# A matrix product by two levels of Strassen-Winograd: A's tiles transposed as 32-bit words, two opening pairs stored, a12's product by the second level in more places

## The chip, the core and the metric

The kernel runs on one core of one Trainium2 chip. Its engines work side by side and meet through semaphores: TensorE (PE, matmuls, with weight loads of its own beside them), VectorE (DVE), ScalarE (ACT), GpSimd (POOL, which here issues the DMAs that turn fp32 into fp16) and SyncE (SP, which issues all other DMAs). The time is device microseconds of one execution; the kernel before has a median of 1470.02 us over 3 runs.

## The reference

```python
def reference(a, b, bias):          # a, b: 4096 x 4096 fp32, bias: 4096 fp32
    return np.tanh(np.matmul(a, b) + bias)
```

The kernel computes in fp16 on PE with fp32 sums.

## The kernel before

**Products.** The output is made in four chunks of 1024 columns (`c` = 0 to 3). A row block is 128 rows of A, a *pair* two of them, a *duo* two pairs. Of a pair, the quadrants a11, a12, a21, a22 are one row block by half of k each; a quadrant is a buffer of 16 k-tiles of 128 x 128. The first level makes seven products of a pair instead of eight: P1 = a11 b11, P2 = a12 b21, P3 = s4 b22, P4 = a22 t4, P5 = s1 t1, P6 = s2 t2, P7 = s3 t3, where s1 = a21 + a22, s2 = s1 - a11, s3 = a11 - a21, s4 = a12 - s2 and t1 to t4 are the same kind of sums of B's quadrants. A *plain* product (`product`, line 726) is 16 matmuls of 512 columns per pair, so 32 per duo. A *fine* one (`fine_product`, line 741, called by `fine` and by the class `Fine`) takes the duo's two pairs together and uses the same scheme once more: seven times 8 matmuls of 256 columns, 56 per duo, with sums of its own: y and z of the left tiles on DVE (`fine_left`), f1 to f4 of the right ones (`fine_right`).

**Stages.** The opening multiplies the first eight row blocks (pairs 0 to 3, buffers `o00` to `o71`) by chunk 0 with plain matmuls in an order written out by hand (lines 1468 to 1511): tiles landing by DMA (`land`), PE, results put aside and taken up again by DVE (`take_up`). Then chunk 0 goes through duos 2 to 7 (`run_duo`), which load A by POOL (`natural`). Chunks 1 to 3 have two passes each (`pass_one`, `pass_two`) over all eight duos: P1, P2 and, in chunks 2 and 3, P6 in the first; P7, P6, P5, P4, P3 in the second. `SECONDS` says in how many duos of the first pass P2 (a12's product) is fine. What a first pass leaves for the second goes to DRAM as a state, but for the last duo, whose state stays on chip.

**Where A comes from.** POOL's DMA reads fp32 rows and writes fp16 into `land` or `nat`, with each 32 partitions holding a quarter of k. DVE then transposes 32 x 32 blocks of it (`transpose`, line 455) into k-tiles, so that k lies on the partitions. A left tile of a matmul is 128 neighbouring fp16 elements per partition. Which k goes to which partition must agree with B's rows: `load_b` reads B with rows `dx` apart per partition and `dt` per tile; for the first four k-tiles `dx` is 4, else 1, and `transpose` makes up for it by a separate instruction. The pairs in `early` (4 to 15) are stored in DRAM in chunk 0 as fp16 tiles (`keep`, names in `BASIS`) and fetched by SP afterwards; pairs 0 to 3 are loaded and transposed once more in chunk 1 (`upper`, `others`).

**The order of the work.** A planner (class `Plan`) takes all operations with a guessed duration, ranks them by a due time and lays them out for each engine; PE's order is that of the program, that of DVE, ACT, POOL and SP comes out of the plan, as does the place in SBUF of each buffer (51 large places). An engine works its queue strictly in that order. `soft` makes an operation due at the latest so long after what it needs.

The planner's guesses for DVE and ACT:

```python
def dve(n, emit, reads, writes, wide=False, **kw):
    add("DVE", 0.15 + n / (960 if wide else 1900), emit, reads, writes, **kw)
def act(n, emit, reads, writes, **kw):
    add("ACT", 0.17 + n / 1200, emit, reads, writes, **kw)
```

Of the kernel before, what the change touches and what calls it, by code (L numbers as in the profile page):

```python
# [10 lines left out]
P = 128  # L11
QP = 32
# [3 lines left out]
T = 16  # L16
TB = 4
# [4 lines left out]
fp16 = mybir.dt.float16  # L22
ADD = mybir.AluOpType.add
# [14 lines left out]
LATER = 6  # L38
PLAIN = (0, 0, 0, 0)
# [4 lines left out]
SECONDS = (0, 4, 6, 8)  # L44
# [81 lines left out]
class Plan:  # L126
    LATE = 0.1
# [235 lines left out]
def kernel(  # L363
# [91 lines left out]
    def transpose(dst, src, h=1, t0=0):  # L455

        nt = src.shape[-1] // QP
        split = [(0, nt, "P mb (t x) -> P mb t x")]
        if h == 0 and t0 == 0:
            split = [(0, TB, "P mb (x t) -> P mb t x"), (TB, nt - TB, split[0][2])]  # L460
        for t, n, order in split:
            nc.vector.transpose(  # L462
                dst[:, ds(t, n), :].rearrange("P t (mb p) -> P mb t p", p=QP),
                src[:, :, ds(t * QP, n * QP)].rearrange(order, x=QP),
            )

    def turn_time(n, h=1, t0=0):
        return (0.34 if h == 0 and t0 == 0 else 0.17) + n * 0.00103
# [11 lines left out]
    def natural_rows(pair, r, s, soft=SOFT):  # L480

        pq = [s.setdefault(f"a{r + 1}{h + 1}", new(f"a{r + 1}{h + 1}", [P, T, P], atoms=2)) for h in range(2)]
        for u in range(2):
            tl = new("nat", [P, 2, 2 * T * QP])

            def srcs(q, u=u):
                src = a[ds((2 * pair + r) * P + u * 2 * QP, 2 * QP), ds(q * KQ, KQ)]
                return src.rearrange("(mb p) k -> p mb k", p=QP), ()

            load_rows(tl, srcs, P * T * P * 4)  # L490
            for h, dst in enumerate(pq):

                def emit(dst=dst, tl=tl, u=u, h=h):
                    transpose(dst[ALL, ALL, ds(u * 2 * QP, 2 * QP)], tl[ALL, ALL, ds(h * T * QP, T * QP)], h)

                add("DVE", turn_time(1024, h), emit, (tl,), ((dst, (u,)),), soft=soft)

    def natural(pair, kept, own=False, few=False):
        s = {}
        for name in ("a11", "a22", "a21", "a12") if few else ():  # L500
            r, h = int(name[1]) - 1, int(name[2]) - 1
            tl = new("nat", [P, 4, T * QP])
            s[name] = new(name, [P, T, P], atoms=2)

            def srcs(q, r=r, h=h):
                src = a[ds((2 * pair + r) * P, P), ds(q * KQ + h * T * QP, T * QP)]
                return src.rearrange("(mb p) k -> p mb k", p=QP), ()

            load_rows(tl, srcs, P * T * P * 4)
            for u in range(2):  # L510

                def emit(dst=s[name], tl=tl, u=u, h=h):
                    transpose(dst[ALL, ALL, ds(u * 2 * QP, 2 * QP)], tl[ALL, ds(2 * u, 2), ALL], h)

                add("DVE", turn_time(1024, h), emit, (tl,), ((s[name], (u,)),))
        for r in () if few else range(2):
            natural_rows(pair, r, s, 0.0)
# [46 lines left out]
    def asum(s, name, x, y, op, over=None):  # L564
        x, y = s[x], s[y]
        s[name] = s[over] if over else new(name, [P, T, P], atoms=2)
        tt(at(s[name]), at(x), at(y), op, T * P, (x, y), (s[name],), wide=False)
# [1045 lines left out]
```

## Time and profile before

| what | value |
|---|---|
| time of 3 runs | 1470.02 us (median), 1469.94 to 1472.13 us |
| the profiled execution | 1469.58 us |
| its span on the core | 1467.9 us |
| granted TensorE clock, mean | 0.998 |
| DMA | 394.33 MB, mean 269 GB/s |
| HBM | 321.39 MB read, 146.54 MB written |

Lines of the profile name an instruction by the line of the program, its engine, its operation and the tiles that it writes and reads (buffer numbers left out). All sums on DVE have line 427, all copies on ACT line 430, the DMAs of A on POOL line 476, those of B line 660, DVE's transposes line 462. "xN" is a count, "mean ns" the mean of one.

### The profile page before, as it was taken

The page shows a single profiled execution, that of the slowest core. Times are in us where ns is not written, and L with a number is a line of the kernel's source. Part 1 is how long each engine was busy: PE and PEld are TensorE (multiplying, and loading weights), DVE is VectorE, ACT ScalarE, POOL GpSimd, SP SyncE. Part 2 cuts the span into 40 slices and gives each one's busy share as a digit, 9 for nine tenths or more (in the row PEclk, how much of TensorE's full clock was granted, in tenths as well). Part 3 has the DMA queues.
Part 4 walks back from the last instruction along what each step waited for, and adds up shares of the span by engine and source line. Part 5 has one row for each costly group of instructions (what it writes and reads, how often), then busy time and mean ns, then how long its engine had stood idle before and what let it go on. Part 6 is the DMA issues. An engine that isn't in the chain of part 4 may idle for free.

```text
span 1467.9 us, 28245 instructions
## 1 busy us (share of the span) xinstructions
PE 1454.4 (99%) x10848; PEld 1060.9 (72%) x10848; DVE 1174.2 (80%) x1835; ACT 439.7 (30%) x990; POOL 310.8 (21%) x581
## 2 busy tenths in 40 slices
PE   9999999999999999999999999999999999999998
PEld 4444545555478566667778878888888888888887
DVE  4669897778688978888789889887778878987765
ACT  2111211221123222433334322244343332243433
POOL 8764334334333011200120300000111210000000
PEclk9999999999999999999999999999999999999999
DMA  9999999999999999999999999588999988778772
GB/s 177 179 220 268 200 255 259 230 229 246 233 274 309 315 281 321 325 340 353 312 289 379 286 327 319 188 295 275 270 291 357 264 239 271 247 233 284 250 252 102
DMA packets 201751, 394.33 MB, mean 269 GB/s; under 512 B 27408, under 2 KB 74512, under 8 KB 201616
## 3 DMA queue, kind: packets, MB, share of 16 engines
q1 hardware_dynamic: 126864, 316.99, 61.7%
q0 software_dynamic: 74752, 75.53, 32.5%
q8 instruction: 85, 1.39, 0.4%
q14 instruction: 50, 0.41, 0.1%
HBM read 321.39 MB, written 146.54 MB: 319 GB/s over the span
## 4 chain that ended last, share of the span: by engine, by line
PE 94%; DMA 3%; POOL 2%; DVE 1%; issue 1%; ACT 0%; DVEq 0%; POOLq 0%; SPq 0%
PE ps L748 60%; PE ps L733 29%; PE ps L1417 5%; DMA b<-in_b_dram 1%; POOL b L660 1%; DMA a<-a 1%; POOL land L476 1%; DMA out_dram<-cs 0%; DMA land<-in_a_dram 0%; DMA out_dram<-parts 0%; POOL first L1344 0%; DVE parts L427 0%; DVE ps L427 0%; DVE t L427 0%; DVE ya L427 0%
## 5 line engine op out<-in xcount | busy, mean ns | idle before, releaser
L660 POOL DMA_DIRECT2D b<-in_b_dram x256 | 137.5, 542 | 560.1 <-DVE ps L427 198.0
L476 POOL DMA_DIRECT2D nat<-in_a_dram x256 | 136.2, 537 | 303.7 <-PE ps L748 91.2
L430 ACT COPY ps<-ps 128x256 f32<-128x256 f32 (+1 forms) x257 | 94.2, 366 | 329.0 <-PE ps L748 316.4
L733 PEld LDWEIGHTS <-s 128*128 128x128 f16 x1056 | 103.3, 98 | 115.9
L462 DVE STREAM_TRANSPOSE a<-nat 128x256 f16<-128x256 f16 (+2 forms) x192 | 155.2, 859 | 30.3 <-PE ps L733 18.8
L733 PEld LDWEIGHTS <-a 128*128 128x128 f16 x896 | 87.4, 98 | 100.5 <-DVE a L427 0.8
L748 PEld LDWEIGHTS <-a 128*128 128x128 f16 x1320 | 129.2, 98 | 25.4 <-issue 1.4
L733 PE MATMUL ps<-b,a 128*128 128x512 f16 x640 | 143.6, 379 | 0.0
L748 PEld LDWEIGHTS <-zs 128*128 128x128 f16 x1248 | 122.1, 98 | 16.0
L748 PEld LDWEIGHTS <-ys 128*128 128x128 f16 x1248 | 122.1, 98 | 14.1
L733 PE MATMUL ps<-t,s 128*128 128x512 f16 x576 | 129.2, 379 | 0.0
L748 PEld LDWEIGHTS <-ya 128*128 128x128 f16 x1136 | 111.1, 98 | 14.8 <-DVE ya L427 1.5
L748 PEld LDWEIGHTS <-za 128*128 128x128 f16 x1136 | 111.2, 98 | 13.7 <-issue 0.2
L430 ACT COPY parts<-ps 128x256 f32<-128x256 f32 (+1 forms) x166 | 65.0, 392 | 171.1 <-PE ps L748 86.9
L1417 PE MATMUL ps<-b,o 128*128 128x512 f16 x512 | 113.1, 383 | 2.4 <-DVE ps L427 2.3
L733 PE MATMUL ps<-b,s 128*128 128x512 f16 x480 | 110.9, 379 | 0.0
L427 DVE TENSOR_TENSOR parts<-ps,parts 128x256 f32<-128x256 f32 (+1 forms) x156 | 68.9, 442 | 43.2 <-PE ps L748 28.4
L448 ACT ACTIVATE parts<-ps 128x512 f32<-128x512 f32 x64 | 38.2, 597 | 201.6 <-PE ps L733 135.2
L1417 PEld LDWEIGHTS <-o 128*128 128x128 f16 x512 | 50.3, 99 | 63.8 <-issue 5.1
L427 DVE TENSOR_TENSOR ps<-ps,parts 128x256 f32<-128x256 f32 (+1 forms) x171 | 76.2, 447 | 21.8 <-PE ps L748 16.8
L748 PE MATMUL ps<-b,a 128*128 128x256 f16 x656 | 85.0, 273 | 1.1 <-ACT ps L430 1.1
L748 PEld LDWEIGHTS <-xs 128*128 128x128 f16 x736 | 72.0, 98 | 10.1 <-issue 1.2
(118 smaller groups left out, 2478.3 us busy)
## 6 DMA issues: line engine op xcount, KB each, us to landing
a<-a SPq DMA_DIRECT2D x74, 512.0 KB, 7.0
a<-a SPq DMA_DIRECT2D x148, 256.0 KB, 6.5
b<-in_b_dram POOLq DMA_DIRECT2D x256, 128.0 KB, 7.6
nat<-in_a_dram POOLq DMA_DIRECT2D x256, 128.0 KB, 7.5
out_dram<-parts SPq DMA_DIRECT2D x112, 256.0 KB, 5.8
ys<-s SPq DMA_DIRECT2D x46, 512.0 KB, 4.5
xs<-s SPq DMA_DIRECT2D x46, 512.0 KB, 5.1
s<-s SPq DMA_DIRECT2D x38, 512.0 KB, 5.9
```

The costliest lines, as they stand in the source:

```text
L427: dve(n, lambda: nc.vector.tensor_tensor(out=o(), in0=x(), in1=y(), op=op), reads, writes, wide, **kw)
L430: act(n, lambda: nc.scalar.copy(o(), x()), reads, writes, **kw)
L448: act(NB, lambda: nc.scalar.activation(o[ALL], src[ALL], TANH), (src,), (o,), soft=2.0)
L462: nc.vector.transpose(dst[:, ds(t, n), :].rearrange("P t (mb p) -> P mb t p", p=QP), src[:, :, ds(t * QP, n * QP)].rearrange(order, x=QP),)
L476: nc.gpsimd.dma_start(out=tl[(ds(q * QP, QP), *key)], in_=src)
L660: nc.gpsimd.dma_start(out=dst.rearrange("p t j n -> p t (j n)") if j is None else dst, in_=src)
L733: nc.tensor.matmul(bank[ALL], left[ALL, k + t, ALL], rb.tile(t), start=start and k == t0 and t == 0, stop=k + t == t0 + nt - 1, skip_group ...
L748: nc.tensor.matmul(bank[ALL, HALF[half]], buf[ALL, at_ * TP + i * TB + t, ALL], rb.tile(t), start=False, stop=i == 1 and t == TB - 1, skip ...
L1417: nc.tensor.matmul(bank[ALL], left[ALL, t, ALL], rb.tile(tb), start=start, stop=stop, skip_group_check=True,)
```

## The change

1. `transpose` looks at the fp16 source as 32-bit words, pairs of neighbouring k, and transposes words. Two k-tiles then lie interleaved in the buffer: word m of a partition holds element m of the one tile and element m of the next. One instruction does what took two in the first half of k; every transpose has half as many elements, of twice the width. A left tile is 128 fp16 elements at a step of two (`left_tile`). `load_b` reads all of B with rows four apart per partition, and the opening's copies behind PE's transposes write at a step of two (`pairs_of`).
2. `natural` always loads a quadrant at a time, which before it did for the first three duos; the later ones had whole rows of k.
3. After the opening, s1 and s2 of pairs 0 and 1 (`FIRST`) are formed from the opening's buffers and a11, a12, a22, s2 are stored in DRAM. In chunk 1 these pairs are fetched as the others are.
4. `SECONDS` goes from (0, 4, 6, 8) to (0, 8, 8, 8): the P2 of four more duos in chunk 1 and two more in chunk 2 is fine.
5. The planner's guesses: DVE's fixed part 0.15 to 0.08, ACT's 0.17 to 0.09, a transpose from 0.17 + 0.00103 n (0.34 where there were two) to 0.09 + 0.00052 n, the time between engines (`LATE`) 0.1 to 0.18.
6. `HOLD` says how many states stay on chip, one in each chunk. `third` would form s3 again from a22 and s2 for pairs whose s3 is not in `held_names`; `others` enters it there for every pair.

```diff
-SECONDS = (0, 4, 6, 8)
+SECONDS = (0, 8, 8, 8)
+HOLD = (1, 1, 1, 1)
+FIRST = (0, 1)
+HELD = ("s1", "s3", "s4")
 class Plan:
-    LATE = 0.1
+    LATE = 0.18
...
-        add("DVE", 0.15 + n / (960 if wide else 1900), emit, reads, writes, **kw)
+        add("DVE", 0.08 + n / (960 if wide else 1900), emit, reads, writes, **kw)
-        add("ACT", 0.17 + n / 1200, emit, reads, writes, **kw)
+        add("ACT", 0.09 + n / 1200, emit, reads, writes, **kw)
...
+    def transpose(dst, src, t0=0, row0=0):
+        src = src.bitcast(pair32)
+        nu, nmb = src.shape[-1] // QP, src.shape[1]
+        nc.vector.transpose(
+            dst[ALL].rearrange("P t m -> P (t m)").bitcast(pair32).rearrange("P (U m) -> P U m", m=P)[
+                :, ds(t0 // 2, nu), ds(row0, nmb * QP)
+            ].rearrange("P (v u) (mb p) -> P mb v u p", p=QP, u=2),
+            src.rearrange("P mb (v x u) -> P mb v u x", x=QP, u=2),
+        )
+    def turn_time(n):
+        return 0.09 + n * 0.00052
+    def pairs_of(buf, t):
+        return buf[ALL, ds(t, 2), ALL].rearrange("P a b -> P (a b)").rearrange("P (m e) -> P e m", e=2)
+    def left_tile(buf, t):
+        return pairs_of(buf, t - t % 2)[:, t % 2]
...
     def load_b(buf, c, k0, nt, j=None, early=0.0):
-        dx, dt = (1, QP) if k0 >= TB else (TB, 1)
...
+                    ap=[[TB * N, QP], [N, nt], [1, n]],
...
-                        bank[ALL], left[ALL, k + t, ALL], rb.tile(t),
+                        bank[ALL], left_tile(left, k + t), rb.tile(t),
...
-                        bank[ALL, HALF[half]], buf[ALL, at_ * TP + i * TB + t, ALL], rb.tile(t),
+                        bank[ALL, HALF[half]], left_tile(buf, at_ * TP + i * TB + t), rb.tile(t),
...
-                eng, 0.35, lambda t=t, fn=fn: fn(aq[m, 0][ALL, ds(t, 2), ALL], box["tp"][:, ds(t, 2), :]),
+                eng, 0.35, lambda t=t, fn=fn: fn(pairs_of(aq[m, 0], t), box["tp"][:, ds(t, 2), :]),
...
+    for p in FIRST:
+        s = {f"a{r + 1}{h + 1}": aq[2 * p + r, h] for r in range(2) for h in range(2)}
+        asum(s, "s1", "a21", "a22", ADD, soft=2.0)
+        asum(s, "s2", "s1", "a11", SUB, over="s1", soft=2.0)
+        keep(p, s)
     finish_bias(k0)
...
-    early = {4, 5, 6, 7, 8, 9, 10, 11, 12, 13, 14, 15}
+    early = set(range(4, NP)) | set(FIRST)
...
-            d.a = [natural(p, p in early, i == 0, i < 3) for p in d.pairs]
+            d.a = [natural(p, p in early, i == 0) for p in d.pairs]
```

More of the change, by code (lines that the diff above doesn't have):

```diff
@@ L22 @@
 fp16 = mybir.dt.float16
+pair32 = mybir.dt.uint32
 ADD = mybir.AluOpType.add
@@ L518, in natural @@
+    def natural(pair, kept, own=False):
+        s = {}
+        for name in ("a11", "a22", "a21", "a12"):
+            natural_tile(pair, name, s)
         if own:
```

133 lines of the change are left out of this document (70 added, 63 removed).

## The prediction

> **What bounds the kernel now.** I read the page first: its span, the engines' busy times and the chain that ended last.
>
> ```profile
> span 1467.9 us, 28245 instructions
> ...
> PE 1454.4 (99%) x10848; PEld 1060.9 (72%) x10848; DVE 1174.2 (80%) x1835; ACT 439.7 (30%) x990; POOL 310.8 (21%) x581
> ...
> PE 94%; DMA 3%; POOL 2%; DVE 1%; issue 1%; ACT 0%; DVEq 0%; POOLq 0%; SPq 0%
> ```
>
> TensorE (PE) is busy 99% of the span and owns 94% of the chain, so the time is PE's work plus its few waits. The chain in order of time gives the pace of that work, and the waits of PE name who ended each of them (us in total, times, longest).
>
> ```profile
> 615.76 6.91 PE ps L733 x32
> 628.75 12.23 PE ps L748 x112
> ```
>
> ```profile
> PE ps L1417 <- DVE ps L427: 2.3, 1, 2.3
> PE ps L748 <- DVE ps L427: 1.6, 3, 0.8
> ...
> PE ps L748 <- DVE ya L427: 1.3, 1, 1.3
> PE ps L748 <- ACT ps L430: 1.1, 1, 1.1
> ```
>
> 32 plain matmuls of 512 columns (line 733) take 6.91 us, 216 ns each; 112 matmuls of 256 columns (line 748, the second level) take 12.23 us, 109 ns each. Nothing stands between them: weight loads are hidden. Two things can move the time: the count of matmuls, and about 6.3 us of waits, of which one, 2.3 us, is in the opening and 4.0 us (1.6 + 1.3 + 1.1) in the rest.
>
> **The change part by part.**
>
> *a12's product.* A duo's plain product is 32 matmuls, 6.91 us; by the second level it is 56, half of 12.23, 6.12 us. Chunk 1 goes from 4 to 8 such duos, chunk 2 from 6 to 8: six duos of 0.79 us, **-4.75 us**. Nothing hides PE, so this comes off the end unless new waits eat it.
>
> *Strided weights.* Every left tile is now read at a step of two elements, and each matmul has a load of its own. Today the loads have step one, except in the sixteen opening transposes on PE, whose source is read at a step of four:
>
> ```profile
> L748 PEld LDWEIGHTS <-a 128*128 128x128 f16 x1320 | 129.2, 98 | 25.4 <-issue 1.4
> ```
>
> ```profile
> L1455 PEld LDWEIGHTS <-first x16: 111/113/137, 9.1 to 11.4; 128*128 128x128 f16 x16
> ```
>
> ```profile
> 9.80 0.41 PE L1455 MATMUL tp<-ident,first 128*128 128x128 f16 x4 [0.30 <-DMA first<-in_a_dram]
> ...
> 10.05 0.59 PE L1417 MATMUL ps<-b,o 128*128 128x512 f16 x2
> ```
>
> A load takes 98 ns dense and 113 ns at step four, and 113 is more than the 109 ns of a 256-column matmul. But four such loads with four 128-column matmuls go from 9.80 to 10.05, 62 ns a pair: the loads overlap each other. A pair at 62 ns fits into 109. Price between 0 and +4 ns x some 8,680 small matmuls, 35 us; I take 0, since 62 ns is a rate and 113 only a latency. The page "TensorE: Matmul & The Clock Gate" of the Trainium skill (section "Weight-path perf modes — Fast Weight Load (FWL) and DoubleRow") says that the fast load reads 32 bits at a time, which speaks against a step that uses one half of each word, and elsewhere allows strided columns. By the first reading the loads would lose their speed and the 35 us rival below would come; the row at step four, which uses a quarter of each 8 bytes, bears out the second.
>
> *Transposes as words.* VectorE (DVE) now moves half as many elements, by one instruction where two were.
>
> ```profile
> L462 DVE STREAM_TRANSPOSE a<-nat 128x1024 f16<-128x1024 f16 x64 | 76.7, 1217 | 11.1 <-PE ps L733 9.5 <-PE ps L748 1.3
> ...
> L427 DVE TENSOR_TENSOR parts<-ps,parts 128x256 f32<-128x256 f32 x144 | 60.7, 422 | 40.7 <-PE ps L748 28.4 <-ACT ps L430 4.9 <-ACT cs L1086 4.4
> L462 DVE STREAM_TRANSPOSE a<-nat 128x768 f16<-128x768 f16 x64 | 59.9, 935 | 0.0
> ...
> L427 DVE TENSOR_TENSOR st<-st,p 128x512 f32<-128x512 f32 x48 | 32.5, 686 | 1.1
> ...
> L427 DVE TENSOR_TENSOR ya<-ya,a 128x1024 f16<-128x1024 f16 x41 | 28.2, 689 | 1.0
> ...
> L462 DVE STREAM_TRANSPOSE a<-nat 128x256 f16<-128x256 f16 x64 | 27.1, 424 | 19.2 <-PE ps L733 9.3 <-DMA nat<-in_a_dram 5.9 <-PE ps L748 3.9
> ...
> L462 DVE STREAM_TRANSPOSE o<-land 128x2048 f16<-128x2048 f16 x8 | 18.1, 2294 | 3.5 <-DMA land<-in_a_dram 2.3 <-PE ps L1417 1.2
> ...
> L462 DVE STREAM_TRANSPOSE o<-land 128x512 f16<-128x512 f16 x12 | 7.5, 680 | 11.3 <-DMA land<-in_a_dram 11.3
> ...
> L1461 DVE COPY o<-tp 128x256 f16<-128x256 f16 x4 | 1.0, 286 | 9.1 <-PE tp L1455 9.1
> ```
>
> No row has a transpose of words. 512 words lie between 424 ns (the 256-element row, if two words went at once) and 1217 ns (1024 half-words, if bytes counted). I take 680: 512 elements of either width take that, transposed (680) or added (686). The 192 transposes of `nat` (76.7 + 59.9 + 27.1 = 163.7 us) become 112 of 0.68, 76 us; the eight long ones of the opening fall from 2294 to the 1217 of 1024 elements, 9 us less. DVE gets some 96 us back, but it is off the chain: worth only what its waits cost. The copies behind PE's transposes (286 ns) now write at step two; at the pace of the 424 row two of them take 0.3 us more, before 12 us, and the stage paced by loads that follows (below) hides it.
>
> *DVE's new work.* Each new fine product costs four half-tile sums (0.69), two bank sums (0.42) and two adds of the state (0.69): 5.0 us, 30 us for six. ACT gets four copies more a duo, at 30% busy (page). The two pairs' s1 and s2 are four sums of 2048 elements, twice the 1024 row or 5.5 us at most, in the opening.
>
> *The opening.* PE's 2.3 us wait is here.
>
> ```profile
> 51.85 2.37 DVE L462 STREAM_TRANSPOSE o<-land 128x1024 f16<-128x1024 f16 x2 [1.37 <-DMA land<-in_a_dram]
> 54.15 4.87 DVE L427 TENSOR_TENSOR ps<-spill,bias 128x512 f32<-128x512 f32 x8
> ```
>
> ```profile
> 40.00:60.00 20.00, 17.67 (x75) 7.50 (x73) 9.54 (x12) 4.20 (x8) 15.71 (x29) 0.91 1.24 185
> ```
>
> (Columns of a stretch: its length, busy time of PE, weight loads, DVE, ACT and POOL, the granted clock of PE, DMA.) The first take-up of a bank (54.15) stands behind two transposes that wait for a landing at 51.85. In the changed kernel's instruction order that take-up comes ahead of them, so the wait should go, and with it the slow clock behind it: 0.91 granted over 20 us, 1.8 us. Together at most 4.1 us. Against it stand the stores of the two pairs: 4 MB on SP, of which 1 MB (a11 of row blocks 0 and 2) leaves around the bias load, before some 45 us.
>
> ```profile
> 80.99 1.58 POOL L660 DMA_DIRECT2D b<-in_b_dram  x3 [0.73 <-DMA b<-in_b_dram]
> ...
> 88.34 5.11 POOL L476 DMA_DIRECT2D land<-in_a_dram  x8 [0.18 <-issue]
> ...
> 103.63 0.54 POOL L476 DMA_DIRECT2D nat<-in_a_dram  x1 [0.81 <-DMA nat<-in_a_dram]
> ```
>
> ```profile
> b<-in_b_dram POOLq DMA_DIRECT2D x256, 128.0 KB, 7.6
> ...
> out_dram<-parts SPq DMA_DIRECT2D x112, 256.0 KB, 5.8
> ```
>
> ```profile
> 92.15 0.60 ACT L448 ACTIVATE parts<-ps 128x512 f32<-128x512 f32 x1 [35.58 <-PE ps L1417]
> ```
>
> POOL's queue of loads paces this stage. From 88.34 eight loads go at 0.64 us each; at 103.63, while outputs of 256 KB are stored, one takes 0.81 + 0.54 = 1.35. So a 256 KB store costs the loads up to 0.7 us, 1 MB 2.8 us. The last block of b is issued by 82.57 and, at the median of 7.6 us, lands by 90; PE is through with its first use at 92.15, when ACT gets the first result. That is 2 us of slack: of the 4.1 gained, less 2.8 lost, little is left. The other 3 MB leave between 90 and 120 us beside the first duo's loads, up to 8 us of their time.
>
> ```profile
> 131.59 2.36 DVE L462 STREAM_TRANSPOSE a<-nat 128x1024 f16<-128x1024 f16 x2
> ```
>
> ```profile
> 139.43 13.98 PE L733 MATMUL ps<-t,s 128*128 128x512 f16 x64
> ```
>
> a22 of the second pair is transposed by 133.95, and the product that needs its sums begins at 139.43, its second half 3.5 us later: some 6 to 9 us of slack less two sums (2.5), which the stores may use up. Then PE waits for s2. So the opening gives between -4.1 and +3 us; nearer to the gain, since the wait that goes is a row and the stores may find gaps, I take **-1.5**. SP issues in order: its bias load now stands behind the first store, which waits for row block 0's transposes, and the bias is first read at 54.15; outputs behind a later store wait for the sums that it waits for, and their buffers come back later to ACT, which is 30% busy. Both I cost at nothing.
>
> *Fewer loads in chunk 1, and what does nothing.* Pairs 0 and 1 come back from DRAM as half-words: 32 POOL loads of 128 KB go, and SP's load issues take their place. Smaller rows in the loads of the first chunk's last three duos (2 KB for 4 KB) and other row steps in the loads of b are hidden: PE's waits name no load behind the opening. I cost them at nothing; without that cover one load late is 1.35 us. One state on chip per chunk is what there was, and no pair meets the condition under which s3 would be formed again.
>
> *Order.* The plan's costs are new, so DVE's order moves everywhere. Chunk 1 is where it could hurt:
>
> ```profile
> 440.00:460.00 20.00, 20.00 (x186) 17.91 (x184) 19.04 (x31) 8.39 (x20) 6.81 (x13) 1.00 1.10 329
> 460.00:480.00 20.00, 20.00 (x178) 17.17 (x176) 16.48 (x26) 6.43 (x15) 7.05 (x13) 1.00 1.14 289
> 480.00:500.00 20.00, 18.75 (x127) 12.06 (x125) 18.74 (x25) 5.40 (x10) 1.62 (x3) 1.00 1.03 313
> 500.00:520.00 20.00, 20.00 (x94) 9.05 (x93) 18.14 (x26) 4.57 (x9) 0.00 (x0) 1.00 0.95 316
> 520.00:540.00 20.00, 20.00 (x142) 13.72 (x141) 11.04 (x17) 5.08 (x12) 1.30 (x3) 1.00 0.82 300
> ```
>
> ```profile
> 408.30 4.74 DVE L462 STREAM_TRANSPOSE a<-nat 128x256 f16<-128x256 f16 x6
> ```
>
> DVE is busy 16.5 to 19.0 of 20 us from 440 to 520. Four new products add 20 us there, while the transposes of pairs 0 and 1, from 408.30, leave. The nearest row for a pass with every a12 by the second level is chunk 3's:
>
> ```profile
> 1137.86 1.03 PE L748 MATMUL ps<-f4b,xa 128*128 128x256 f16 x8 [0.77 <-DVE ps L427]
> ```
>
> 0.77 us is the longest wait in it. New waits lie between -4.0 (all of today's gone) and +10 (below); I take **+0.7**, that row.
>
> **Sum.** Profiled time 1469.58 (span 1467.9 and 1.7 around it): 1469.58 - 4.75 - 1.5 + 0.7 = 1464.0. The median shown, 1470.02, is 0.44 above that execution; the forecast is 1464.4, call it **1464**.
>
> **The rivals.**
>
> *DVE becomes the bound late in chunk 1's first pass (slower).* From 460 to 520 DVE has 53.4 of 60 us; plus 20 for four products, 73 us in 57 of PE time. What is over, 16 us, must go ahead into 400 to 460, where leaving transposes make room, or behind, into 520 to 540 (11.04 busy, 9 us free). If only half finds room, PE waits 8 to 10 us for t2, t3 and the y/z sums: 1464 + 9 = 1473. For: today's 1.3 us wait on `ya` falls in this pass. Against: 19.04 of 20 from 440 to 460 runs without a wait. It decides from about 6 us of waits on; below that it only eats gain.
>
> *The gains are eaten (no change).* Opening +2 and waits +3 leave 1470. For: the store traffic falls on the one stage paced by loads. Against: the transposes give time back there.
>
> *Opening and waits both clear.* -4.1 in the opening and -2 of the 4.0: 1469.6 - 4.75 - 6.1 + 0.4 = 1459.
>
> *Strided loads are not hidden.* +35 us: 1499. For: 113 against 109. Against: 62 ns a pair.
>
> **How the numbers follow.** A change of less than 0.2% (2.9 us, 1467.1 to 1472.9) can't be told from none. Chances: forecast with its own range 1461 to 1467, 0.60; both clear 0.13; eaten 0.12; DVE bound 0.11; strided loads 0.04. Faster: 0.60 + 0.13 and a third of the eaten, 0.77. Same: the rest of it and a little of the DVE case, 0.11. Slower: 0.12. The range that should hold 8 in 10 takes in most of "both clear" and "eaten": 1459 to 1471.
>
> **What would show it.** In the profile of the changed kernel: line 748's matmuls still 12.23 us for 112 and PE's matmul count 144 higher (336 of 256 columns more, 192 of 512 fewer); load latency between 98 and 113 ns; word transposes of 512 near 680 ns and DVE near 1110 us; no PE wait at 52 us and a clock of 1.00 from 40 to 60; PE's waits named DVE below 4 us between 400 and 560. Wrong would be: a 256-column pace above 110 ns, a PE wait for b near 85 us or for s2 near 135 us over 2 us, DVE at 20 of 20 around 500 us with PE waiting.

## The result and the profile after

| | median | runs | range |
|---|---|---|---|
| before | 1469.89 us | 12 | 1466.97 to 1472.13 |
| after | 1473.57 us | 12 | 1470.49 to 1479.16 |

The ratio is 1.0033, with a 95% interval of 1.0019 to 1.0046: the changed kernel is slower, by 3.7 us in the medians and 4.8 by the ratio. Its profiled execution took 1470.86 us, near its fastest; a second one, profiled later, took 1474.48 us, near the median, and is used beside it. First the page of the changed kernel: the span, the busy times and the chain that ended last.

```profile
span 1469.1 us, 28503 instructions
...
PE 1450.6 (99%) x10992; PEld 1074.8 (73%) x10992; DVE 1096.6 (75%) x1799; ACT 447.5 (30%) x1014; POOL 296.2 (20%) x549
...
PE 79%; DMA 6%; DVE 3%; issue 1%; ACT 0%; POOL 0%; SPq 0%; DVEq 0%; POOLq 0%
```

TensorE has its 144 matmuls more, VectorE 78 us less work, and yet it is not faster. (The chain after can be followed back only to 135 us of the span, so its shares add up to 89% and 79 does not stand against 94; transfers have 6% of the span for 3, VectorE 3% for 1.) TensorE's own pace is what it was, as a piece of the chain in order of time and the groups kept apart by shape show (mean ns behind the busy time):

```profile
532.25 12.23 PE ps L744 x112
```

```profile
L744 PEld LDWEIGHTS <-a 128*128 128x128 f16 x1440 | 140.9, 98 | 30.4 <-issue 5.2
```

```profile
L463 DVE STREAM_TRANSPOSE a<-nat 128x512 uint32<-128x512 uint32 x112 | 72.7, 687 | 41.1 <-PE ps L729 30.7 <-PE ps L744 4.8 <-DMA nat<-in_a_dram 4.7
...
L463 DVE STREAM_TRANSPOSE o<-land 128x1024 uint32<-128x1024 uint32 x8 | 9.9, 1243 | 18.2 <-DMA land<-in_a_dram 16.7 <-DMA s<-s 1.5
```

What has grown are TensorE's waits (us in total, times, longest):

```profile
PE ps L744 <- DVE ps L431: 4.7, 7, 1.2
PE ps L729 <- DVE s L431: 4.6, 2, 2.6
PE ps L744 <- ACT ps L434: 1.8, 2, 1.1
PE warm L1367 <- DVE zeros L1361: 1.4, 1, 1.4
PE ps L729 <- DVE a L431: 0.5, 1, 0.5
```

The wait of 2.3 us in the opening is gone. New are 4.6 us for `s`, and the waits for VectorE's writes into banks went from 1.6 to 4.7 us. In stretches (length, busy PE, weight loads, DVE, ACT, POOL, granted clock, DMA share, GB/s):

```profile
40.00:60.00 20.00, 20.00 (x94) 9.09 (x93) 9.60 (x14) 4.01 (x8) 14.63 (x27) 1.00 1.25 210
120.00:140.00 20.00, 17.94 (x84) 8.02 (x83) 17.10 (x25) 3.03 (x6) 9.34 (x18) 1.00 1.16 277
140.00:160.00 20.00, 17.42 (x82) 7.73 (x81) 19.50 (x37) 2.45 (x4) 9.32 (x18) 1.00 1.14 264
440.00:460.00 20.00, 19.88 (x182) 17.55 (x181) 11.88 (x21) 7.38 (x18) 7.57 (x14) 1.00 1.00 254
460.00:480.00 20.00, 18.98 (x175) 16.86 (x173) 16.30 (x28) 7.00 (x16) 8.71 (x16) 1.00 1.13 272
480.00:500.00 20.00, 20.00 (x185) 17.93 (x184) 19.05 (x30) 8.40 (x20) 5.45 (x10) 1.00 1.12 307
500.00:520.00 20.00, 18.81 (x154) 14.80 (x152) 18.82 (x26) 6.46 (x16) 0.00 (x0) 1.00 0.98 328
```

From 40 to 60 us TensorE is full and its clock 1.00, where it had 17.67 us and 0.91. From 120 to 160 it loses 4.6 us, where it lost none.

To add such losses up I use one measure below: the time from the start of each matmul to the start of the next, less the pace of its kind (215.8 ns for 512 columns, 109.2 for 256, 55.8 for 128), summed over a stretch. It holds waits and slow clock together. Before: 7.7 us in 0 to 200 us, none from 200 to 400, 5.0 behind 400. After: 9.1, none and 9.9; in the second execution 9.6, none and 13.0. With the 4.75 us that the fine products save, after comes out at -4.75 + 1.4 + 4.9 = +1.5 us in the first execution (the spans differ by 1.2) and -4.75 + 1.9 + 8.0 = +5.2 in the second (4.9). So the saving is there in full, and both other terms have turned against it. All of this compares single executions; what is chance between them comes up below.

**The first duo.** VectorE makes s1 and s2 of the first duo from tiles that POOL loads. Its queue in the profile after, and the loads of `nat` issued from 93 to 130 us, before and after:

```profile
122.19 1.31 DVE L463 STREAM_TRANSPOSE a<-nat 128x512 uint32<-128x512 uint32 x2
...
127.83 1.31 DVE L463 STREAM_TRANSPOSE a<-nat 128x512 uint32<-128x512 uint32 x2 [2.46 <-DMA nat<-in_a_dram]
...
136.25 1.23 DVE L431 TENSOR_TENSOR s<-s,a 128x2048 f16<-128x2048 f16 x1
...
142.45 1.23 DVE L431 TENSOR_TENSOR s<-s,a 128x2048 f16<-128x2048 f16 x1
```

```profile
L476 POOL DMA_DIRECT2D nat<-in_a_dram x32: 542/542/545, 93.6 to 128.4; - x32
...
DMA to landing us min/median/max: 6.1/8.4/12.4
```

```profile
L487 POOL DMA_DIRECT2D nat<-in_a_dram x25: 542/545/545, 94.3 to 129.5; - x25
...
DMA to landing us min/median/max: 7.9/11.2/12.8
```

32 loads have become 25 in the same stretch, and each lands 11.2 us after its issue instead of 8.4. The sums end at 137.5 and 143.7 us; TensorE waits 2.1 and 2.6 us for them.

**Behind 400 us.** The two executions of the changed kernel at the same place, VectorE's queue:

```profile
499.00 1.28 DVE L431 TENSOR_TENSOR t<-t,t 128x1024 f16<-128x1024 f16 x2
501.22 1.23 DVE L431 TENSOR_TENSOR b<-b,b 128x2048 f16<-128x2048 f16 x1 [0.93 <-DMA b<-in_b_dram]
502.36 0.42 DVE L431 TENSOR_TENSOR parts<-ps,parts 128x256 f32<-128x256 f32 x1
502.69 1.22 DVE L431 TENSOR_TENSOR t<-b,t 128x2048 f16<-128x2048 f16 x1
503.82 0.42 DVE L431 TENSOR_TENSOR ps<-ps,parts 128x256 f32<-128x256 f32 x1
```

```profile
502.63 1.23 DVE L431 TENSOR_TENSOR b<-b,b 128x2048 f16<-128x2048 f16 x1 [2.86 <-DMA b<-in_b_dram]
...
505.24 0.42 DVE L431 TENSOR_TENSOR ps<-ps,parts 128x256 f32<-128x256 f32 x1
```

VectorE stands until a block of b has landed. Behind it in the queue are a sum of b and the two adds (`parts`, `ps`) that bring a bank to the state in which TensorE's next fine product goes on. TensorE loses 1.35 us here in the first execution and 3.28 in the second: VectorE's stand is 1.93 us longer in the second, and so is TensorE's loss. VectorE is not full (16 to 19 of 20 us from 460 to 520, 11.9 from 440 to 460); its queue has the wrong thing at its head. TensorE's list of waits names VectorE; the landing is one step further back. The first execution loses 0.4 us or more at nine places behind 400 us. Two of them (1.26 us at 410 and 0.69 at 1462) are in every run of this document, the kernel before included. At the other seven, 6.4 us together, VectorE has stood on a transfer at most 8 us earlier.

### The profile page after: what moved, and what is told of

It reads as the page before. It is cut to its first block, busy times and chain, and to the rows that moved or that the text cites. A ratio compares the mean times of both kernels' runs of the same rounds, so it can differ in the third digit from the quotient of the medians.

```text
span 1469.1 us, 28503 instructions
## 1 busy us (share of the span) xinstructions
PE 1450.6 (99%) x10992; PEld 1074.8 (73%) x10992; DVE 1096.6 (75%) x1799; ACT 447.5 (30%) x1014; POOL 296.2 (20%) x549
## 4 chain that ended last, share of the span: by engine, by line
PE 79%; DMA 6%; DVE 3%; issue 1%; ACT 0%; POOL 0%; SPq 0%; DVEq 0%; POOLq 0%
PE ps L744 55%; PE ps L729 24%; DMA b<-in_b_dram 3%; DMA s<-a 1%; DMA state<-st 1%; DVE parts L431 1%; DMA nat<-in_a_dram 0%; DVE ps L431 0%; DVE s L431 0%; DMA out_dram<-parts 0%; DMA a<-a 0%; DVE zs L431 0%; DVE st L431 0%; DVE ya L431 0%; DVE za L431 0%
## 5 line engine op out<-in xcount | busy, mean ns | idle before, releaser
L487 POOL DMA_DIRECT2D nat<-in_a_dram x224 | 121.1, 546 | 249.0 <-PE ps L729 83.7
L744 PEld LDWEIGHTS <-a 128*128 128x128 f16 x1440 | 140.9, 98 | 30.4 <-issue 5.2
L729 PE MATMUL ps<-t,s 128*128 128x512 f16 x608 | 137.0, 379 | 4.6 <-DVE s L431 4.6
L744 PEld LDWEIGHTS <-zs 128*128 128x128 f16 x1248 | 122.1, 98 | 16.1
L744 PEld LDWEIGHTS <-za 128*128 128x128 f16 x1232 | 120.5, 98 | 15.3 <-issue 1.2
L744 PEld LDWEIGHTS <-ya 128*128 128x128 f16 x1232 | 120.6, 98 | 14.4
L729 PE MATMUL ps<-b,s 128*128 128x512 f16 x512 | 118.5, 379 | 0.0
L729 PEld LDWEIGHTS <-a 128*128 128x128 f16 x640 | 62.5, 98 | 74.2 <-DVE a L431 1.0
L463 DVE STREAM_TRANSPOSE a<-nat 128x512 uint32<-128x512 uint32 x112 | 72.7, 687 | 41.1 <-PE ps L729 30.7
L744 PE MATMUL ps<-b,a 128*128 128x256 f16 x720 | 93.3, 273 | 1.2 <-ACT ps L434 1.1
L729 PE MATMUL ps<-b,a 128*128 128x512 f16 x416 | 92.6, 379 | 0.5 <-DVE a L431 0.5
L452 ACT ACTIVATE parts<-ps 128x512 f32<-128x512 f32 x52 | 31.1, 598 | 167.3 <-PE ps L729 105.2
```

The costliest lines, as they stand in the source:

```text
L452: act(NB, lambda: nc.scalar.activation(o[ALL], src[ALL], TANH), (src,), (o,), soft=2.0)
L463: nc.vector.transpose(dst[ALL].rearrange("P t m -> P (t m)").bitcast(pair32).rearrange("P (U m) -> P U m", m=P)[:, ds(t0 // 2, nu), ds(row ...
L487: nc.gpsimd.dma_start(out=tl[(ds(q * QP, QP), *key)], in_=src)
L729: nc.tensor.matmul(bank[ALL], left_tile(left, k + t), rb.tile(t), start=start and k == t0 and t == 0, stop=k + t == t0 + nt - 1, skip_grou ...
L744: nc.tensor.matmul(bank[ALL, HALF[half]], left_tile(buf, at_ * TP + i * TB + t), rb.tile(t), start=False, stop=i == 1 and t == TB - 1, ski ...
```

## The experiments

Ratios are to runs of the kernel before on the same chip, with 95% intervals. "Loss" is the measure above, in the profiled execution, for 0 to 200 us and behind 400. "Stands" is the time that VectorE was idle between 400 and 1260 us with a DMA named as what ended it, and how often, summed over the rows of its list of waits. Two cautions: a stand is not a loss, since not every stand reaches TensorE (run 4 has the most stands and loses 8.8 us behind 400, run 17 has 15.6 and loses 18.5); and the loss is of one execution, which in run 4 was the fastest of twelve (1469.17 us, median 1473.49).

| run | words | two pairs stored | a12 fine in | costs for the order | other | ratio | loss | stands |
|---|---|---|---|---|---|---|---|---|
| before | no | no | 4, 6, 8 | old | | 1 | 7.7, 5.0 | 12.0, 15 |
| after | yes | yes | 8, 8, 8 | new | | 1.0033 (1.0019 to 1.0046) | 9.1, 9.9 | 31.7, 22 |
| after, second | yes | yes | 8, 8, 8 | new | | one time | 9.6, 13.0 | 26.9, 19 |
| 1 | yes | no | 8, 8, 8 | new | | 1.0028 (1.0018 to 1.0037) | 3.6, 15.8 | 33.6, 26 |
| 2 | yes | yes | 4, 6, 8 | new | | 1.0041 (1.0029 to 1.0053) | 10.6, 7.8 | 33.4, 27 |
| 3 | no | no | 8, 8, 8 | old | | 1.0104 (1.0089 to 1.0119) | 5.3, 29.3 | 18.7, 13 |
| 4 | yes | no | 4, 6, 8 | new | | 1.0021 (1.0009 to 1.0033) | 3.6, 8.8 | 35.3, 31 |
| 5 | yes | yes | 8, 8, 8 | old | | 1.0112 (1.0098 to 1.0125) | 7.2, 25.9 | 30.9, 18 |
| 6 | yes | yes | 8, 8, 8 | new | all loads 2 us later | 1.0052 (1.0038 to 1.0066) | 16.1, 9.6 | 29.6, 26 |
| 7 | yes | no | 8, 8, 8 | new | all loads 2 us later | 1.0059 (1.0046 to 1.0072) | 11.1, 14.6 | 13.6, 14 |
| 9 | yes | no | 4, 6, 8 | old | | 0.9998 (0.9989 to 1.0007) | 3.6, 9.8 | 16.6, 15 |
| 10 | no | no | 4, 6, 8 | new | | 1.0025 (1.0014 to 1.0036) | 5.2, 8.9 | 31.3, 21 |
| 11 | yes | later | 8, 8, 8 | new | | 1.0009 (1.0000 to 1.0017) | 7.6, 11.5 | 22.9, 19 |
| 12 | yes | later | 8, 8, 8 | new | loads of chunks 1 to 3 | 0.9995 (0.9986 to 1.0003) | 9.6, 9.5 | 25.7, 17 |
| 13 | yes | no | 4, 6, 8 | new | loads of chunks 1 to 3 | 1.0016 (1.0008 to 1.0025) | 3.9, 11.1 | 20.8, 17 |
| 14 | yes | no | 4, 6, 8 | old | loads of chunks 1 to 3 | 0.9989 (0.9981 to 0.9998) | 3.0, 7.2 | 7.7, 14 |
| 15 | yes | one pair | 8, 8, 8 | new | loads of chunks 1 to 3 | 0.9993 (0.9983 to 1.0004) | 5.6, 9.7 | 21.4, 18 |
| 16 | yes | yes | 8, 8, 8 | new | loads of chunks 1 to 3 | 1.0010 (1.0000 to 1.0019) | 10.7, 8.8 | 24.3, 20 |
| 17 | no | no | 4, 6, 8 | old | loads of chunks 1 to 3 | 1.0094 (1.0079 to 1.0109) | 5.5, 18.5 | 15.6, 8 |
| 18 | yes | one pair | 4, 6, 8 | old | loads of chunks 1 to 3 | 1.0069 (1.0056 to 1.0081) | 3.7, 18.8 | 28.4, 19 |

Any edit gives the planner's whole order anew, so a run tells its part with a noise of its own, some us behind 400; what is read from it is what shows in the place where it should.

**The change taken apart (runs 1 to 4).** Of the changed kernel, in turn, the stores, the fine products, and both are undone; run 3 does the fine products alone on the kernel before.

```diff
# runs 1 and 4
-FIRST = (0, 1)
+FIRST = ()
# runs 2 and 4
-SECONDS = (0, 8, 8, 8)
+SECONDS = (0, 4, 6, 8)
# run 3, on the kernel before
-SECONDS = (0, 4, 6, 8)
+SECONDS = (0, 8, 8, 8)
```

Expected of runs 1 to 4, in this order:

> The changed kernel without the two pairs that go to DRAM in the opening (FIRST empty, everything else as changed). Theory A: the 4 MB of extra stores share the 16 DMA engines with the loads of A for the first duo; in the profile of the changed kernel the sixteenth load of nat lands at 127.4 us against 119.6 before, and TensorE waits 2.2 and 2.7 us for s2 at 135 and 141 us and 0.6 us at 184. Without the stores that load lands near 120 us, the three waits go, the opening keeps its even pace at 52 us, and the profiled span is 1469.1 - 5.5 = 1463.6 us, less up to 1 us for what pairs 0 and 1 now load again as natural rows. Rival B: the waits come from the order of the new transposes and sums on VectorE; then they stay within 1 us of 5.5 and the span is 1468 to 1471.

> The changed kernel with a12's product fine in as many duos as before (SECONDS 0, 4, 6, 8). 144 fewer matmuls, +4.75 us of TensorE's nominal pace. Theory A: the waits at 456 to 504 us, 782 to 787 and 1160 us (about 6 us in the profile of the changed kernel, against 1.5 in those places before) belong to the six more fine products and fall to about 1.5: span 1469.1 + 4.75 - 4.4 = 1469.4 us. Rival B: they belong to the new order of all work (new costs for the order, tiles loaded one by one) and stay: 1473.9 us.

> The kernel before with only a12's product fine in all eight duos of chunks 1 and 2 (SECONDS 0, 8, 8, 8): half-word transposes, no stores in the opening, costs for the order as before. VectorE has 30 us more work. TensorE's nominal pace is 4.75 us shorter. Theory A: the fine products bring waits of about 4.4 us with them where loads land close to their use: 1467.9 - 4.75 + 4.4 = 1467.5 us, the waits behind 400 us by name on VectorE's adds into the banks. Rival B, the waits come from the new order: 1463.2 us. If VectorE's spare time matters (chunk 1's first pass, where it would be over full with slow transposes), 1470 or more.

> The changed kernel without the opening's stores and with a12's product as before: what is left is the word transposes, tiles loaded one by one, b's even steps and the new costs for the order. Theory A: the opening's 52 us wait and slow clock are gone (-4.1 us), the waits at 135 to 184 us are gone, those of the extra fine products too: 1467.9 - 4.1 = 1463.8 us. Rival B (order): 1467 to 1473 us, with waits behind 400 us of 5 us or more.

Run 1 without the stores, the same stretch of loads and TensorE's stretches:

```profile
L487 POOL DMA_DIRECT2D nat<-in_a_dram x32: 542/542/545, 92.8 to 129.1; - x32
...
DMA to landing us min/median/max: 6.2/8.5/11.7
```

```profile
40.00:60.00 20.00, 20.00 (x94) 9.10 (x93) 10.66 (x15) 4.11 (x8) 16.47 (x31) 1.00 1.25 195
120.00:140.00 20.00, 20.00 (x95) 9.04 (x94) 17.41 (x28) 3.72 (x7) 9.99 (x19) 1.00 1.15 278
140.00:160.00 20.00, 20.00 (x94) 9.05 (x93) 16.95 (x33) 2.48 (x5) 9.20 (x17) 1.00 1.16 269
```

The loads are back at 32 and 8.5 us, the waits for s2 are gone, and the loss in the opening is 3.6 us: theory A holds there, and the opening's two halves are now separate. Without the stores the opening loses 7.7 - 3.6 = 4.1 us less than before; the stores take 9.1 - 3.6 = 5.5 back.

The 4.1 us are not the words' alone. Of the kernel before's 7.7, 2.5 are the wait at 52 us and 1.7 the slow clock behind it. Runs 3 and 17 transpose half-words and have the same order here: they lose 1.7 and 2.1 us at that place, and no slow clock follows (5.3 and 5.5 in the whole opening). Run 10 transposes half-words too, in the order of the new costs, and has no wait there at all. Runs 17 and 10:

```profile
40.00:60.00 20.00, 18.11 (x85) 8.13 (x84) 11.01 (x13) 4.20 (x8) 16.24 (x31) 1.00 1.25 193
```

```profile
40.00:60.00 20.00, 20.00 (x94) 9.11 (x93) 12.59 (x15) 4.01 (x8) 16.11 (x30) 1.00 1.24 188
```

So the wait goes with the order of VectorE's queue, with words or without, and the slow clock was there in the profiled execution of the kernel before and not in these two. What the words and their loads give beyond the new order is at most the 1.6 us between run 10 (5.2) and run 4 (3.6), in single executions.

The total of run 1 did not follow (1.0028): behind 400 us run 1 loses 15.8 us, 5.9 of them between 750 and 1000 us, where the changed kernel lost 1.5: another order, with other places.

Runs 2 and 1 show what is left of the fine products' 4.75 us. By the ratios they bring 0.0008 (run 2 against after, 1.2 us) with the stores, and cost 0.0007 (run 4 against run 1) without, both well inside the intervals. In run 2 the waits at 456 to 504 and at 782 to 787 us went, as theory A said, but others came (1.8 us at 831, 1.0 at 1123), and the span, 1473.2 us, is the one that rival B gave. Run 4 came out as rival B said: a span of 1467.5, with 8.8 us lost behind 400. Run 3 shows them on the kernel before, 15 us slower. Its VectorE queue and the stretch around it:

```profile
492.28 1.23 DVE L427 TENSOR_TENSOR b<-b,b 128x2048 f16<-128x2048 f16 x1 [3.02 <-DMA b<-in_b_dram]
493.42 0.68 DVE L427 TENSOR_TENSOR ya<-a 128x1024 f16<-128x1024 f16 x1
494.14 0.69 DVE L427 TENSOR_TENSOR ya<-ya,a 128x1024 f16<-128x1024 f16 x1
```

```profile
480.00:500.00 20.00, 11.40 (x81) 8.98 (x82) 13.90 (x19) 2.85 (x7) 0.54 (x1) 0.83 0.84 259
```

TensorE waits 7.2 us for `ya`, from 487.7 to 494.9. For 3.0 of them VectorE stands until a block of b has landed; for the other 4.2 it works, on sums that come before `ya` in its queue and on `ya`. From 478 to 489 us it works with pauses of at most 0.4 us, and brings the `ya` before that one late as well (2.3 us of wait at 479). Of the three cases of the expectation only the last, 1470 or more, held, and its reason in part: over 20 us VectorE is not full, over these 11 it nearly is.

**Is it the costs for the order? (runs 5, 9, 10).**

```diff
# runs 5 and 9, on the changed kernel (9 with the edits of run 4); run 10 the other way, on the kernel before
-    LATE = 0.18
+    LATE = 0.1
-        add("DVE", 0.08 + n / (960 if wide else 1900), emit, reads, writes, **kw)
+        add("DVE", 0.15 + n / (960 if wide else 1900), emit, reads, writes, **kw)
-        add("ACT", 0.09 + n / 1200, emit, reads, writes, **kw)
+        add("ACT", 0.17 + n / 1200, emit, reads, writes, **kw)
```

Expected of runs 5, 9 and 10, in this order:

> The changed kernel, its work ordered with the costs of before (0.15 and 0.17 us instead of 0.08 and 0.09 a VectorE and ScalarE operation, 0.1 instead of 0.18 us of lateness). Theory C: behind 400 us VectorE's queue stands on a load that has not landed (b at 467.9 and 501.2 us, a at 781.0, xa at 1158.7, idle 0.9 to 2.1 us before each) and the adds into the banks that TensorE needs next stand behind it; the new costs put these operations closer to the landing. With the old costs the waits behind 400 us fall from 7.2 to about 3 us: span 1465 us, ratio to before 1.000. Rival D: the costs do not matter, the places only move: span 1468 to 1472, ratio 1.002 to 1.004.

> The changed kernel without the opening's stores, with a12's product as before and with the old costs for the order: what is left is the word transposes, tiles loaded one by one and b's even steps. The same with the new costs took 1.0021 of the time before. If the new costs eat the 4.1 us of the opening (theory E: they put VectorE's work on a landed tile too early, ahead of the adds into the banks), the ratio is 0.997 to 0.998 and the profiled span near 1464 us. If the word tiles or the loads themselves do (theory F), it stays at 1.001 to 1.004, span 1467 to 1470.

> The kernel before with the new costs for the order alone (0.08, 0.09, 0.18). Theory E: slower, 1.001 to 1.004, with more waits behind 400 us for VectorE's adds into the banks. Theory F: within 0.001 of before, span 1466 to 1469.

With nothing else changed, the new costs make the kernel before slower by 0.0025, 3.7 us, and VectorE's stands go from 12.0 to 31.3 us; between runs 9 and 4, the same pair of costs with words, 0.0023 and 16.6 to 35.3. So theory E holds for these two pairs, though run 9 stays short of the 0.997 to 0.998 that it gave. It fails for the whole change: run 5, with the old costs, is the slowest of the changed kernel's kin and above both cases of its expectation. Its largest losses are 5.8 us at 803 us, where VectorE stands 4.1 us until a store of `ya` has landed, and 2.3 at 502, where it stands 2.5 us for b. Not all of it is transfers: at 543 and 956 us TensorE loses 2.5 and 2.8 us while VectorE works without a pause. The first of these two:

```profile
540.00:550.00 10.00, 8.10 (x64) 6.01 (x63) 10.00 (x17) 1.00 (x3) 1.83 (x4) 1.00 0.78 280
```

Neither set of costs is the better one by itself.

Run 9 is also the transposes as words with nothing but the loads that go with them. The opening's 4.1 us are there (loss 3.6) and the kernel is no faster. The largest place is this line of its VectorE queue:

```profile
429.17 0.71 DVE L463 STREAM_TRANSPOSE a<-nat 128x512 uint32<-128x512 uint32 x1 [3.60 <-DMA nat<-in_a_dram]
```

TensorE loses 2.75 us at 428 us, and 1.6 more by a slow clock behind it.

**Later landings in the plan (runs 6, 7, 12 to 14, 16, 17), later stores (11), one pair (15, 18).**

```diff
# runs 6 and 7 (7 without the stores)
-DMA = {"POOL": (380e3, 3.75), "in": (405e3, 3.1), "out": (315e3, 2.8)}
+DMA = {"POOL": (380e3, 5.75), "in": (405e3, 5.1), "out": (315e3, 2.8)}
# runs 12 to 18
     for c in range(NC):
+        if c == 1:
+            DMA.update({"POOL": (380e3, 5.75), "in": (405e3, 5.10)})
# runs 11 and 12: the opening's keep(p, s) put off
         for i, pairs in enumerate(duos):
+            for p, s in opened if i == 1 else ():
+                keep(p, s, after=plan.last_pe)
# runs 15 and 18
-FIRST = (0, 1)
+FIRST = (0,)
```

Expected of runs 6 and 7, of the second execution of the changed kernel, and of runs 11 and 12, in this order:

> The changed kernel, its work ordered as if each load took 2 us longer to land (5.75 instead of 3.75 us for POOL's loads, 5.1 instead of 3.1 for SP's); nothing else. Theory C: work on a landed tile is put later in VectorE's queue, and the adds into the banks ahead of it; waits behind 400 us fall from 7.2 to about 2 us, the opening's 5.6 us at 135 to 184 us stay (its loads are late by 8 us, not 2): span 1464 us, ratio 0.999. Rival D: 1468 to 1472, ratio 1.002 to 1.004.

> As the run with later loads, and without the two pairs' stores in the opening. Theory C with theory A: no wait at 135 to 184 us and about 2 us behind 400: span 1460 us, ratio to before 0.996. Rival D: 1467 to 1472, ratio 1.001 to 1.004.

> The changed kernel once more, for a second profile: 1470.5 to 1479 us were its times. If the places of the waits are set by the order, the same ones show again within 0.5 us each (135 and 141 us: 5.0 in all; 471, 503, 782 to 787, 1160 us). If they are chance, others show.

> The changed kernel, the eight opening tiles' stores issued only after TensorE's last product of the first duo (about 185 us) instead of from 91 us on; all else as changed. Theory A: the loads for the first duo land near 120 us, the waits at 135 and 141 us (5.0 us) go, and what the stored tiles save later is kept: span 1469.1 - 5.0 = 1464.1, ratio 0.9995 to 1.0005 by the medians. If the eight tiles held longer, or the stores at 185 us, make the second or third duo wait instead (rival): 2 to 5 us of waits between 180 and 260 us and no gain, 1.002 to 1.004.

> As the run with later stores, and the work of the chunks 1 to 3 ordered as if each load took 2 us longer (the opening and chunk 0 as changed). In the run where that held for the opening too, the waits behind 400 us came to 9.6 us of TensorE's pace against 9.9 and 13.0 in two executions of the changed kernel. If later assumed landings help there: 1 to 3 us less than the run with later stores, span 1461 to 1463, ratio 0.998 to 0.999. If the landing does not decide: the same as that run within 1 us.

Runs 6 and 7 came out above both cases: with later landings for the opening too, its loads are ordered worse (16.1 and 11.1 us lost there). The second execution of the changed kernel told what is fixed and what is not: the waits for s2 came again within 0.4 us (1.89 and 2.74 against 2.23 and 2.74), the loss at 502 us more than doubled.

Run 11 takes the stores out of the first duo's way: median 8.4 us to landing again, and a ratio of 1.0009 instead of 1.0033, some 3.5 us. It is not free. The eight tiles are stored from 165.5 to 173.4 us and hold their places until then, and the next duo pays, as the rival said, with 2.8 us (that it is the places which it waits for is argued, not shown); the stretch of run 11:

```profile
160.00:200.00 40.00, 37.53 (x202) 19.34 (x201) 29.18 (x51) 7.83 (x15) 10.81 (x20) 1.00 0.99 292
```

Expected of runs 13 to 18, in this order:

> The changed kernel without the opening's stores and with a12's product as before (new costs; 1.0021 of the time before), the work of chunks 1 to 3 ordered as if each load took 2 us longer. Theory G: the waits at 428 and 819 us (2.1 and 1.5 us) fall below 0.7 us each, ratio 0.998 to 1.000, span 1464 to 1466. Rival H: 1.001 to 1.004.

> The same with the old costs for the order (0.9998 without the later landings). Theory G: the wait at 428 us (2.8 us) falls below 1 us, ratio 0.997 to 0.999, span 1464 to 1466. Rival H: 0.999 to 1.003.

> The changed kernel with one opening pair stored instead of two (FIRST is pair 0 alone, 2 MB of stores instead of 4) and landings of chunks 1 to 3 assumed 2 us later. If the wait for s2 goes with the bytes stored (theory A): the loads for the first duo land near 123 us, the waits at 135 and 141 us come to 0 to 2 us instead of 5.0, ratio 0.998 to 1.000. If it stays at 4 us or more: 1.001 to 1.003.

> The changed kernel, all of it, with landings of chunks 1 to 3 assumed 2 us later and nothing else. Theory G: the opening's waits of 5.0 us at 135 and 141 us stay, the wait at 502 us (1.4 and 3.3 us in two executions) falls below 0.7 us, ratio 1.001 to 1.002 against 1.0033. Rival H: 1.002 to 1.005.

> The kernel before, the work of chunks 1 to 3 ordered as if each load took 2 us longer; nothing else. If the later landings alone make the gain of the run with words and old costs (0.9989), this one is at 0.998 to 1.000 too and the words bring nothing. If the words' shorter opening (4.0 us less excess there) is what remains once the waits behind 400 us are smaller, the words are needed: this one at 1.000 to 1.003, its opening as before (2.3 us of waiting at 52 us).

> The run with words, old costs and later landings (0.9989), and one pair of the opening stored (2 MB of stores) so that its tiles need not be transposed again in chunk 1. If the stores cost at 135 to 147 us what they save behind 400 us: within 0.001 of 0.9989. If the tiles saved count more: 0.997 to 0.998, and the wait at 773 us (1.9 us) is under 1 us.

Later landings for chunks 1 to 3 alone seem to have helped the changed kernel (run 16, 1.0010 against 1.0033, intervals that meet at 1.0019; the loss at 497 us was still 1.7, so not in the way theory G said) and, by 0.0014 with intervals that touch, run 12 against run 11; they did nothing that can be told for run 13 against run 4: the waits at 428 and 819 us went, as theory G said, and others came (2.8 us at 1122, 1.3 at 1086). With words and old costs (run 14) the stands fell from 16.6 to 7.7 us, the wait at 428 us went, and the kernel is faster than before, 0.9989 with an interval that ends at 0.9998. TensorE's waits in run 14:

```profile
PE ps L744 <- DVE ps L431: 2.5, 5, 1.0
PE ps L744 <- DVE ya L431: 2.1, 2, 1.7
```

Run 15 bears out theory A by its size: half the stores, loads landing in 9.3 us (median), 1.2 us lost from 100 to 150 instead of 5.0, 0.9993 in all. But the late loads do not make the wait by themselves. In the order of the old costs, run 5 stores both pairs, its loads land in 11.2 us, and it loses 2.2 us from 100 to 150; run 18 stores one pair, its loads land in 10.9, and it loses nothing there. So the 5.5 us of the stores belong to the order of the new costs; by the old ones they are 7.2 - 3.6 = 3.6 (run 5 against run 9).

Runs 17 and 18 forbid a simple ending; both came out above every case of their expectations. The same edit that goes with run 14's gain costs the kernel before 14 us, and one stored pair on top of run 14 costs 12 us. In both the largest place is at the change from chunk 1 to 2: 10.6 us in run 18, nearly all that it loses on run 14, and 8.2 in run 17. Run 17 loses another 5.0 from 485 to 490, where VectorE works with no pause above 0.2 us on sums that come before `ya`. VectorE's queue and the stretch in run 18:

```profile
787.00 0.68 DVE L431 TENSOR_TENSOR f1b<-b 128x1024 f16<-128x1024 f16 x1
795.95 0.69 DVE L431 TENSOR_TENSOR f2b<-b,f1b 128x1024 f16<-128x1024 f16 x1 [8.26 <-DMA a<-ya]
796.56 0.68 DVE L431 TENSOR_TENSOR ya<-ya,a 128x1024 f16<-128x1024 f16 x1
```

```profile
780.00:800.00 20.00, 9.78 (x75) 7.61 (x74) 11.53 (x22) 5.47 (x12) 4.35 (x8) 0.79 1.13 306
```

The store named, as the trace shows that one instruction:

```profile
L533 SPq DMA_DIRECT2D a<-ya x1: 320/320/320, 783.8 to 783.8; - x1
...
DMA to landing us min/median/max: 12.0/12.0/12.0
```

`f2b` is to be written where a `ya` still lies whose store to DRAM was issued at 783.79 us and landed at 795.83, 12.0 us later, in a queue of SP's that at that time lands one transfer every 1.3 to 2.0 us. The planner takes a store to be through 2.8 us after its bytes have flowed. VectorE stands 8.26 us and TensorE waits 8.2 us for the `ya` behind it. In run 17 VectorE stands 8.2 us for a store of `st`.

## Why the prediction was wrong

- **a12's product, -4.75 us: right.** 144 matmuls more, 12.23 us for 112 of them; the two sums of the result close to 0.3 us with it.
- **Strided weights hidden: right.** Loads take 98 ns at step two, as at step one, and the pace of the matmuls is the same. The reading of the Trainium skill ("TensorE: Matmul & The Clock Gate", section "Weight-path perf modes — Fast Weight Load (FWL) and DoubleRow") by which the loads would lose their speed is not borne out here.
- **Word transposes: right.** 687 ns for 680, 1243 for 1217, VectorE 1097 us for "near 1110".
- **The opening, -1.5 us: wrong, mis-sized.** It measured +1.4 and +1.9. The wait at 52 us went, and by the step named, the order (run 10 shows it without words). Run 1 lost 4.1 us less than the kernel before, the figure that I had, but 1.7 of it was the slow clock, a term taken from a single execution: runs 3 and 17 have the wait and no slow clock. The failed step is the price of the stores: of 2.8 us for b and "some 6 to 9 us of slack less two sums" for the first duo I expected that the stores "may find gaps". They did not: the loads of 93 to 130 us landed 2.8 us later in the median, the slack was used up, and 5.5 us were lost in this order. The text had named the place (s2 near 135 us), the sign and the mechanism, and took the other end of its range. In the Trainium skill, "DMA: Bandwidth & Descriptors" (section "Queues, rings and completion order") has each DMA engine go round robin between the queues that have work; the loads' medians of 11.2 us with the stores and 8.5 without agree with it, and no run here shows the round robin itself.
- **Order and new waits, +0.7 us: wrong, and the largest error.** It measured +4.9 and +8.0. The step that failed is the cover, in the words of the prediction: "PE's waits name no load behind the opening". They seldom can: most of what TensorE multiplies has been transposed or summed by VectorE first (where the lists of other runs name a transfer behind the opening, it is for 0.2 to 1.4 us), so a late load shows as a wait for VectorE (at 502 us, 1.93 us more of a stand on b were 1.93 us more of TensorE's loss). The list of VectorE's own waits would have told that it stood 12.0 us on transfers between 400 and 1260 us already before, with the DMA share at 1.03 to 1.14 in the stretches from 440 to 500 us that I quoted. The price, 0.77 us, was one wait of one order; the row's own stretch, 1120 to 1140 us, had a share of 1.06, so the traffic does not tell it from chunk 1. Run 10 against before and run 4 against 9 show that the new costs bring such stands, some 19 us more of them, with words or without; the words bring 4 to 5. Which of the stands reach TensorE the totals do not tell.
- **The rival "VectorE becomes the bound"** gave 1473 us and the measurement 1473.6, but by another cause: VectorE has 1.0 to 8 us free of each 20 from 440 to 520. Where it has the slow transposes as well, in run 3, both causes show: 3.0 us of the longest wait are a landing and 4.2 are VectorE's own work.
- **The forecast as a whole** put 0.73 on two terms going well at once. Bounds of -4.1 to +3 and -4 to +10 were worked out and held; their middles would have given 1469.58 - 4.75 - 0.5 + 3 = 1467, and the second execution came to +1.9 and +8.0, near both far ends.

Not settled: why later assumed landings went with smaller ratios for three orders (after, 11 and 9; for none of them with intervals clearly apart), did nothing clear for run 4 and cost the kernel before 14 us. At most of the large places a transfer stands at the head of VectorE's queue; at others (runs 3, 5 and 17) VectorE works without a pause and what TensorE needs comes too late in its queue. Which transfer is the last in time changes with every order, and between executions of one kernel (0.93 and 2.86 us at the same block of b). That the order is what the change loses behind 400 us is shown for the costs alone (run 10); for the whole change it is argued from the places. Where time was lost is known only for the profiled executions.

## What to carry to other kernels

When the engine on the chain names another engine in its waits, read that engine's own waits too, and ask what stands at the head of its queue. Here it was the planner's shorter guesses, more than the faster transposes, that brought VectorE to its transfers too early: its stands went from 12.0 to 31.3 us without words and from 16.6 to 35.3 with them. Extra stores are priced by the loads that run beside them, by the slack of what those loads feed and by what waits behind them in the consumer's queue, not by how idle the issuing queue is. Where a planner lays out all queues anew at every edit, a change of a few us in the work can be paid back many times in one place: undo its parts one at a time, and look for the place before believing a total.

## What was not expected of the hardware

- A load of weights at a step of two elements takes 98 ns, as at step one; the one at step four on the kernel before took 113.
- VectorE's transpose takes nearly the same time for an element of 16 or 32 bits: 1217 ns for 1024 half-words, 1243 for 1024 words.
- A slow clock followed some waits and not others of like length. In run 9 a wait of 2.75 us at 428 us was followed, 1.3 us after its end, by 15 matmuls at 212 to 215 ns instead of 109 (clock 0.91 from 420 to 440 us); in the changed kernel's second execution a wait of 3.28 us was followed by none. In run 3, 37 matmuls ran at that pace, 3.9 us on top of the waits: 22 behind a wait of 7.4 us at 487, 15 behind waits of 1.8, 0.2 and 0.4 us from 800 to 803, and none behind one of 2.5 us at 479. At 52 us the kernel before waited 2.5 us and ran slow behind it, run 17 waited 2.1 and did not.
- A store of 256 KB on SP's queue landed 12.0 us after its issue while the queue was full, against a median of 5.9 us for the 22 stores of its kind in that kernel.
